# A hybrid transformer layer on one core: S5's filler products, the moment q and k are asked for, and the place of the W2 block sums

## The chip, the core and the metric

The kernel runs on one core of a Trainium2 chip. TensorE (PE) multiplies; VectorE (DVE), ScalarE (ACT) and GpSimd (POOL) do elementwise work; SyncE (SP) mostly issues transfers. The metric is the device time of one launch in microseconds (us): the median of several runs.

## The reference

One layer of a streaming encoder, 1024 tokens, model width 1024, float32. The parts that matter here:

```
h    = rmsnorm(x)
proj = h @ w_in          # u (512) | conv x, B, C | q, k, v (512 each) | forget (8) | gates (3 x 1024)
y_a  = s5(u)             # 32 groups x 16 channels, complex diagonal scan, GELU, GLU
y_b  = B * conv3(C * x_conv)
y_c  = forgetting_attention(q, k, v, f)          # 8 heads x 64, causal
merged = sum_i sigmoid(gates_i) * (y_i @ w_branch_i)
x = x + rmsnorm(merged @ w_out)
x = x + rmsnorm(square(relu(rmsnorm(x) @ w_ff1)) @ w_ff2)
```

## The kernel before, in words

**Stages.** RMSNorm and transposes of x; the projection u; S5's parameters; S5 itself in four quarters of eight groups; V; attention over four head pairs; branch merge and w_out; the two MLP matrices, each by a scheme of seven products of sums of blocks (t_P1 to t_P7 in DRAM), for which the kernel makes sums of blocks of w_ff1 and w_ff2.

**Products.** A float32 weight tile is split into a high and a low part (`split`: ACT copies the high part, DVE subtracts), and each product is three matmuls 128x512. One filler step is three matmuls; a weight tile of 128 columns is 48 matmuls (two halves of 24), and a raw weight load (`r_...`, 1 MB, two buffers) holds two tiles.

**S5's quarter j** (`s5_quarter`, L703 to L818). DVE makes Bt, POOL makes Bx, DVE adds them; PE transposes the sum (pm); ACT copies (Mi). DVE makes CA, POOL makes Cx, DVE adds (CA); PE multiplies (pk), giving Kq and by eight small copies Wi. PE multiplies (px); DVE multiplies by the tables TR and TI (X), scans (Z, eight scans) and multiplies back (S, with Zs from ACT); PE multiplies S and U (py); GELU on ACT and DVE (G, gq); PE multiplies (pz); ACT and DVE finish (so), SP stores (ya). POOL builds the tables for the next quarter meanwhile, from steps of 8 columns to steps of 512 (`s5_tables`).

**What sets the order.** PE's order is written by generators on an estimated clock, `clk`: every matmul adds its cost. `spawn` puts a generator into a heap, `poll` resumes those whose time has come, and `run_with(filler)` (L114) issues one filler step whenever nothing is due. So a `yield SY * 9.0` in `s5_quarter` says how much filler PE gets before the next step of S5. The filler is `proj_stream` (L263): the conv's tiles (cx, cc, cb), then the gates g0 to g22, and q and k of a head pair when asked for (`request_qk`). The next tile is split when the present one has reached a given step. The other engines' order follows from this order of recording, by a list scheduler for most stages; in attention SP's order is as recorded, and before V that of DVE and ACT.

**V and attention.** V's two groups (`v_group`) run behind S5, with the forget gates' chain (`forget`) beside the second; POOL makes the step matrix `stf` for it. Attention (`attention`, around L1104 to L1126) runs 64 units of 128 queries: scores (ps), softmax on DVE and ACT, transposes (pt), products with V (av), all filled by gates' and q/k products. q and k of the next head pair are asked for at unit 12 of each 16.

**W2 sums** (`w2_sums`, L1131 to L1147). Sixteen times: SP reads 1 MB of w_ff2 into w2s (one buffer), POOL makes four differences of blocks 128x512, SP stores four of 256 KB (t_P). In before it starts together with attention.

## Time and profile before

| | us |
|---|---|
| median of 3 runs | 1651.32 |
| lowest, highest | 1644.12, 1651.83 |
| the profiled execution | 1648.08 |
| its span | 1646.3 |
| PE busy | 1603.7 |
| first pm0 | 94.29 |
| py0, py1, py2, py3 | 146.66, 211.28, 273.31, 334.52 |
| W2 sums: first block's read, last store | 427.0, 734.3 |
| head pairs 1, 2 and 3 of attention begin | 559.7, 656.3, 726.4 |

Times in the profile count from the span's start. A row of the timeline is: start, duration, engine, line, operation, output <- inputs, shapes, count; the bracket at its end is the engine's idle time before it and what ended it. A matmul's duration includes its way through the pipeline: two matmuls 128x512 start 0.23 us apart. PEclk is the clock that PE was granted, 1.00 being full. A line can be that of a helper (L65 is any two-input elementwise step), so tiles tell more than lines.

### The profile page before, as it was taken

To read this page: it belongs to the slowest core of one execution; us is meant where nothing else is said; L and a number is where in the kernel's file an instruction comes from. 1 tells how busy PE (TensorE), PEld (TensorE's weight loads), DVE (VectorE), ACT (ScalarE), POOL (GpSimd) and SP (SyncE) were. 2 spreads that over 40 slices of the span, in tenths; PEclk is the share of its full clock that TensorE was granted. 3 is DMA by queue.
4 is the path that set the end of the run, shared out by engine and by line. 5 is a ranking of instruction groups with operands and counts; after the bars stand their busy time and mean duration, and the time that the engine had idled before them with its cause. 6 is when DMAs were issued, how large, how long until landed. Compare 5 with 4: busy or idle time off the path is not lost.

```text
span 1646.3 us, 20948 instructions
## 1 busy us (share of the span) xinstructions
PE 1603.7 (97%) x7783; PEld 1322.8 (80%) x7783; DVE 1033.7 (63%) x1543; ACT 702.9 (43%) x1060; POOL 460.8 (28%) x578
## 2 busy tenths in 40 slices
PE   7999999999999999999999989999999999999997
PEld 6778888889878888777887768888788878888886
DVE  4768666524156463677682874978887674545665
ACT  6223233322254454566343344744445454443442
POOL 1087844100231413120002314444433200101232
PEclk9999999999999999999999999999999999999999
DMA  5412323332463526441873672456554699665521
GB/s 166 125 46 77 105 76 111 91 103 64 145 214 111 196 96 202 131 167 62 282 253 110 216 241 90 149 173 198 184 175 146 202 344 358 236 202 187 186 88 51
DMA packets 186034, 261.73 MB, mean 159 GB/s; under 512 B 24752, under 2 KB 108764, under 8 KB 183884
## 3 DMA queue, kind: packets, MB, share of 16 engines
q1 hardware_dynamic: 170380, 228.93, 43.2%
q10 hardware_dynamic: 15552, 31.46, 5.1%
q8 instruction: 61, 1.00, 0.2%
q14 instruction: 41, 0.34, 0.1%
HBM read 183.54 MB, written 75.63 MB: 157 GB/s over the span
## 4 chain that ended last, share of the span: by engine, by line
PE 42%; DVE 7%; issue 3%; DMA 3%; ACT 3%; POOL 2%; SPq 0%; DVEq 0%; ACTq 0%; POOLq 0%
PE P L122 13%; PE P4f L122 3%; PE P6f L122 3%; PE P7f L122 3%; PE P5f L122 3%; PE P2f L122 3%; PE P3f L122 3%; PE P1f L122 2%; PE wl L122 2%; PE p_g L122 2%; DVE sa L65 1%; PE p_q L122 1%; PE ps L122 1%; PE av L122 1%; PE pt L126 1%
## 5 line engine op out<-in xcount | busy, mean ns | idle before, releaser
L65 DVE TENSOR_TENSOR st<-x,st 128x1024 fp32r<-128x1024 f32 x70 | 86.8, 1251 | 78.5 <-ACT st L73 77.0
L122 PE MATMUL p_g<-hT,w_g_1H 128*128 128x512 f32 x384 | 125.6, 403 | 0.0
L122 PE MATMUL p_g<-hT,w_g_0H 128*128 128x512 f32 x384 | 124.2, 401 | 1.2 <-ACT K L1019 1.2
L73 ACT ACTIVATE st<-x 128x1024 fp32r<-128x1024 f32 x70 | 73.6, 1059 | 99.0 <-PE P6f L122 16.6
L65 POOL TENSOR_TENSOR w2s<-w2s 128x512 f32<-128x512 f32 x32 | 44.5, 1390 | 215.7 <-DMA w2s<-in_w_ff 188.4
L65 POOL TENSOR_TENSOR s<-w1r 128x512 f32<-128x512 f32 x32 | 53.8, 1701 | 145.5 <-DMA w1r<-in_w_ff 114.9
L65 DVE TENSOR_TENSOR sl<-x,sh 128x1024 fp32r<-128x1024 f32 x42 | 56.6, 1352 | 47.4 <-ACT sh L73 47.4
L122 PEld LDWEIGHTS p_g<-hT,w_g_0H 128*128 128x128 f32 x384 | 69.7, 189 | 13.5 <-ACT K L1019 1.6
L122 PE MATMUL pb<-yH,wb_0L 128*128 128x512 f32 x192 | 75.5, 393 | 3.6 <-DVE wb_0L L65 3.6
L122 PEld LDWEIGHTS p_g<-hT,w_g_1H 128*128 128x128 f32 x384 | 69.4, 190 | 11.6 <-issue 0.2
L122 PE MATMUL p_g<-hT,w_g_1L 128*128 128x512 f32 x192 | 75.8, 395 | 0.0
L122 PE MATMUL p_g<-hT,w_g_0L 128*128 128x512 f32 x192 | 75.5, 393 | 0.0
L65 POOL TENSOR_TENSOR fa<-fa,gfin 128x512 f32<-128x512 f32 x16 | 25.5, 1604 | 178.3 <-ACT fjk L1762 178.3
L122 PE MATMUL pb<-yH,wb_0H 128*128 128x512 f32 x192 | 75.2, 392 | 0.0
L122 PE MATMUL pb<-yL,wb_0H 128*128 128x512 f32 x192 | 74.8, 390 | 0.0
L65 DVE TENSOR_TENSOR PT<-pt,PT 128x512 fp32r<-128x512 f32 (+2 forms) x96 | 53.1, 553 | 28.9 <-ACT PT L73 28.4
L73 ACT ACTIVATE PT<-pt 128x512 fp32r<-128x512 f32 (+2 forms) x96 | 46.9, 489 | 53.5 <-PE pt L126 52.4
L73 ACT ACTIVATE sh<-x 128x1024 fp32r<-128x1024 f32 x42 | 44.2, 1058 | 51.4 <-PE P3f L122 9.9
L1056 ACT ACTIVATE P<-ps,mx 128x128 f32<-128x128 f32 (+3 forms) x64 | 47.3, 739 | 28.1 <-DVE mx L1053 28.0
L1053 DVE TENSOR_REDUCE mx<-ps 128x1 f32<-128x128 f32 (+3 forms) x64 | 48.1, 751 | 13.6 <-PE ps L122 13.3
L862 ACT ACTIVATE g<-p_g,bgcol 128x512 f32<-128x512 f32 x48 | 32.8, 682 | 45.8 <-PE p_g L122 45.3
L126 PE MATMUL pt<-ident,P 128*128 128x128 f32 x288 | 48.7, 278 | 3.0 <-DVE PT L65 2.3
(810 smaller groups left out, 4568.0 us busy)
## 6 DMA issues: line engine op xcount, KB each, us to landing
w2s<-in_w_ff SPq DMA_DIRECT2D x16, 1024.0 KB
w1r<-in_w_ff SPq DMA_DIRECT2D x16, 1024.0 KB
as<-sa SPq DMA_DIRECT2D x16, 1024.0 KB
x<-as SPq DMA_DIRECT2D x32, 512.0 KB
x<-t_P SPq DMA_DIRECT2D x32, 512.0 KB
r_g<-in_w_in SPq DMA_DIRECT2D x12, 1024.0 KB
gt_s<-g ACTq DMA_DIRECT2D x48, 256.0 KB
t_P<-w2s SPq DMA_DIRECT2D x48, 256.0 KB
```

The source lines that it names most:

```text
L65: (eng or dve).tensor_tensor(o, x, y, op=op)
L73: act.activation(hi, src, AF.Copy, scale=scale)
L122: pe.matmul(o, l, r, start=start, stop=stop)
L126: pe.transpose(o, i, idn)
L862: act.activation(g, ps, AF.Tanh, bias=bgcol[:, i:i + 1], scale=0.5)
L1053: dve.tensor_reduce(mx, sv, axis=mybir.AxisListType.XY, op=MAX, negate=True)
L1056: act.activation(Pm[:, 0:kend].rearrange("p (c n) -> p c n", c=nch), sv, AF.Exp, bias=mx, accum_out=sm)
```

## The change

1. `run_with` takes a name at which to stop; S5's loop stops when S5 has ended, and later loops poll, so that a generator can go on beside them.
2. S5's yields: 15.0 instead of 9.0 before Bt's add in quarter 0; 8.0 instead of 13.0 (quarter 0) and 1.5 instead of 3.9 (others) before CA's add; 10, 15, 13 and 11 instead of 15 before py.
3. q and k of the next head pair are asked for when the filler left in the present tiles covers the work of the units in front (by durations measured on `clk`), at unit 15 at the latest; such a tile from another raw load is split half a tile later.
4. The W2 sums start in S5's last quarter, behind CA's add (POOL copies one column of CA into the buffer first), make the four differences in place without the second buffer, and pause between V's second group's beginning and the end of `forget`.

The same products and sums are computed. Core of the diff:

```
-        yield SY * (3.9 if j else 9.0)
+        yield SY * (3.9 if j else 15.0)
         tt(Bt, Bt, Bx, ADD)
...
-        yield SY * (3.9 if j else 13.0)
+        yield SY * (1.5 if j else 8.0)
         tt(CA, CA, Cx, ADD)
+        if j == 3:
+            spawn(w2_sums(CA[:, 0, 0, 0:1]))
...
-        yield SY * 15.0
+        yield SY * (10.0, 15.0, 13.0, 11.0)[j]
         py = pp.tile([P, 8, P], F, name=f"py{j}", tag="s", bufs=2)
...
-            if n % 16 == 12 and hp < 3:
+            k = n % 16
+            if k < 8:
+                dur[k] = clk[0] - t0
+            elif hp < 3 and not asked.get(hp) and (k == 15 or ahead_us[0] >= sum(dur[q] for q in range(k - 7, 7))):
+                asked[hp] = True
                 request_qk(hp + 1)
...
+            if i == 0:
+                pool.tensor_copy(w[:, 0, 0, 0:1], after)
+            sp.dma_start(w.rearrange("p k h e -> p k (h e)"), w2_p[:, i])
+            yield 4.5
+            while "v" in ended and "forget" not in ended:
+                yield 1.0
```

How PE's order moves. Counted on it, from one S5 step to the next: 24 more matmuls before pm0; 21 fewer from pm0 to pk0 (51 for 72); 24 fewer from px0 to py0 (78 for 102); 12 fewer from pm to pk in quarters 1 to 3 (21 for 33); px to py 102 as before in quarter 1, 93 for 102 in quarters 2 and 3; 24 for 33 from py3 to pz3. V begins 84 rows earlier, and two tiles (96 matmuls) stand in attention instead: g10 and g12 fill head pair 0, g14 and g16 pair 1, g18 and g20 pair 2. From the second half of the tile q for head pair 3 on, PE, ACT, DVE and SP have the same order in both.

PE around the first transposes, before (p_cc is a conv product, pm S5's transposes of Bt):

```order
322 L122 MATMUL p_cc_00_1103<-hT_172,w_cc_0H 128x512
323 L122 MATMUL p_cc_00_1103<-hT_173,w_cc_0H 128x512
324 L122 MATMUL p_cc_00_1103<-hT_172,w_cc_0L 128x512
325 L126 MATMUL pm_1114<-ident,Bt_1016 128x128 x8
326 L122 MATMUL p_cc_00_1103<-hT_174,w_cc_0H 128x512
327 L122 MATMUL p_cc_00_1103<-hT_175,w_cc_0H 128x512
```

and the same place after:

```order
346 L124 MATMUL p_cc_01_1138<-hT_176,w_cc_0H 128x512
347 L124 MATMUL p_cc_01_1138<-hT_177,w_cc_0H 128x512
348 L124 MATMUL p_cc_01_1138<-hT_176,w_cc_0L 128x512
349 L128 MATMUL pm_1152<-ident,Bt_1019 128x128 x8
350 L124 MATMUL p_cc_01_1138<-hT_178,w_cc_0H 128x512
351 L124 MATMUL p_cc_01_1138<-hT_179,w_cc_0H 128x512
```

The transposes stand 24 rows later, inside the second half of the same weight tile.

DVE in quarter 1, before (X from px, w_cb the split of a weight tile, ac the conv, Z the scans):

```order
282 L65 TENSOR_TENSOR X_1885<-px_1875,TI_1269 64x1024 x2
283 L65 TENSOR_TENSOR X_1884<-px_1875,TR_1268 128x1024
284 L65 TENSOR_TENSOR X_1884<-X_1884,X_1885 128x1024
285 L65 TENSOR_TENSOR w_cb_0L<-r_cb_1953,w_cb_0H 128x1024
286 L65 TENSOR_TENSOR ac_1779<-ac_1779,bs_1906 128x1024
287 L777 SCALAR_TENSOR_TENSOR Z_1912<-r_505,X_1884 128x128 x8
```

and after:

```order
280 L65 TENSOR_TENSOR X_1846<-px_1836,TI_1275 64x1024 x2
281 L65 TENSOR_TENSOR X_1845<-px_1836,TR_1274 128x1024
282 L65 TENSOR_TENSOR X_1845<-X_1845,X_1846 128x1024
283 L65 TENSOR_TENSOR w_cc_0L<-r_cc_1890,w_cc_0H 128x1024
284 L65 TENSOR_TENSOR vp_1829<-vp_1829,xs_1660 128x1024
285 L60 TENSOR_SCALAR ac_1886<-vp_1829,cwcol 128x1024
286 L68 SCALAR_TENSOR_TENSOR ac_1886<-vp_1829,cwcol,ac_1886 128x1024 x2
287 L809 SCALAR_TENSOR_TENSOR Z_1866<-r_505,X_1845 128x128 x8
```

Before, the split of w_cc, the add vp and the conv's three taps stood ahead of X, and two other steps stood between X and the scans; now those five stand between.

POOL behind the last quarter's Cx, after (w2s is a block of w_ff2, stf the step matrix for V):

```order
238 L65 TENSOR_TENSOR Cx_2663<-C2t,pii_515 128x8x16 x9
239 L683 COPY w2s_2692<-CA_2662 128x1
240 L65 TENSOR_TENSOR w2s_2692<-w2s_2692 128x512 x4
241 L65 TENSOR_TENSOR w2s_2827<-w2s_2827 128x512 x4
242 L65 TENSOR_TENSOR w2s_2948<-w2s_2948 128x512 x4
243 L969 MEMSET stf 128x1024
```

Before, Cx was followed by stf at once, and the sums came behind four memsets for attention. On SP's queue the first block's read stands, after, right behind quarter 2's stores and ahead of the load r_g6 and of the eight Wi copies of quarter 3; the load r_wv0 (for V's second group) stands behind the fourth block's read. The last block's stores stand ahead of the load r_q2, so all sixteen blocks are through before head pair 2.

More of the change, by code (lines that the diff above doesn't have):

```diff
@@ L112, in settle, with run_with @@
             poll()
-    def run_with(filler):
-        while events:
+    ended = set()
+    def run_with(filler, until=None):
+        while events and until not in ended:
             if events[0][0] > clk[0] and next(filler, DONE) is DONE:
@@ L261, in proj @@
             yield
+    ahead_us = [0.0]
     def proj_stream():
@@ L282, in proj_stream @@
                 poll()
+            late = nxt is not None and nxt.ready is not None and nxt.raw is not cur.raw
             for th in range(2):
                 for kt, _ in enumerate(proj(cur, th)):
-                    if nxt is not None and (th, kt) == (0, 5):
+                    if nxt is not None and (th, kt) == ((1, 0) if late else (0, 5)):
                         nxt.split()
+                    ahead_us[0] = 0.64 * (15 - 8 * th - kt + 16 * (nxt is not None))
                     yield
@@ L666, in hybrid_layer, with w2_sums @@
     gp = es1.enter_context(pool_("gp", side="right"))
+    w2_es = ExitStack()
+    w2p = w2_es.enter_context(pool_("w2p", side="right"))
+    def w2_sums(after):
+        w2_p = a["w_ff2"].rearrange("(i k p) e -> p i k e", p=P, k=2)
+        for i in range(16):
+            w = w2p.tile([P, 2, 2, HALF], F, name=f"w2s{i}", tag="w2s")
+            if i == 0:
[4 more added lines that the diff above has]
+                yield 1.0
+            b11, b12, b21, b22 = w[:, 0, 0], w[:, 0, 1], w[:, 1, 0], w[:, 1, 1]
+            tt(b11, b12, b11, SUB, pool)
+            tt(b12, b22, b12, SUB, pool)
+            tt(b22, b22, b11, SUB, pool)
+            tt(b21, b21, b22, SUB, pool)
+            yield 6.5
+            for m, src in (("P5", b11), ("P7", b12), ("P6", b22), ("P4", b21)):
+                sp.dma_start(t_s[m][i // 4][:, i % 4], src)
+            yield 3.0
     PX = 5.0
@@ L875, in s5_all @@
             yield from s5_quarter(j)
+        ended.add("s5")
     s5_tables(0)
     spawn(s5_all(), 0)
-    run_with(ps_)
+    run_with(ps_, "s5")
     while any(t.name[0] == "c" for t in todo) or len(todo) > 21:
         next(ps_)
+        poll()
     cv_es.close()
@@ L921, in hybrid_layer @@
             next(ps_)
+            poll()
         split(wv[1][1], wv[1][2], wv[1][0])
@@ L924, in hybrid_layer @@
             next(ps_)
+            poll()
         split(wv[0][1], wv[0][2], wv[0][0])
         for _ in v_group(1):
-            pass
+            poll()
     zfl = zf.rearrange("p t h -> p (t h)")
@@ L979, in forget @@
             sp.dma_start(cum_s[2 + k], cmn[:, k, :])
+        ended.add("forget")
+    ended.add("v")
     spawn(forget(), 1.0)
     vg = v_group(0)
-    run_with(vg)
+    run_with(vg, "forget")
     for _ in vg:
-        pass
+        poll()
     vc_es.close()
@@ L1105, in attention @@
         prev = None
+        dur, asked, t0 = {}, {}, 0.0
         for n, u in enumerate(units):
@@ L1113, in attention @@
                 yield 4.0
+                t0 = clk[0]
             scores(u)
@@ L1119, in attention @@
                 yield from tail(prev)
-            if n % 16 == 12 and hp < 3:
+            k = n % 16
[3 more added lines that the diff above has]
+                asked[hp] = True
                 request_qk(hp + 1)
+            t0 = clk[0]
             prev = u
@@ L1127, in hybrid_layer @@
     FILL_A, FILL_B = 1.1, 0.6
-    def w2_sums():
-        w2_p = a["w_ff2"].rearrange("(i k p) e -> p i k e", p=P, k=2)
-        yield 4.0
-        for i in range(16):
-            w = at.tile([P, 2, 2, HALF], F, name=f"w2s{i}", tag="w2s")
-            t2 = at.tile([P, HALF], F, name=f"w2t{i}", tag="w2t")
-            sp.dma_start(w.rearrange("p k h e -> p k (h e)"), w2_p[:, i])
-            yield 7.0
-            b11, b12, b21, b22 = w[:, 0, 0], w[:, 0, 1], w[:, 1, 0], w[:, 1, 1]
-            tt(b11, b12, b11, SUB, pool)
-            tt(t2, b22, b11, SUB, pool)
-            tt(b12, b22, b12, SUB, pool)
-            tt(b21, b21, t2, SUB, pool)
-            yield 9.0
-            for m, src in (("P5", b11), ("P6", t2), ("P7", b12), ("P4", b21)):
-                sp.dma_start(t_s[m][i // 4][:, i % 4], src)
-            yield 3.0
     with tc.manual_schedule(engines={mybir.EngineType.SP}):
         spawn(attention())
-        spawn(w2_sums())
         run_with(ps_)
     es3.close()
+    w2_es.close()
     ext = ctx.enter_context(pool_("ext"))
```

## The prediction

> **What bounds the kernel now.** I read the page first: it says which engine is full.
>
> ```profile
> span 1646.3 us, 20948 instructions
> PE 1603.7 (97%) x7783; PEld 1322.8 (80%) x7783; DVE 1033.7 (63%) x1543; ACT 702.9 (43%) x1060; POOL 460.8 (28%) x578
> ```
>
> TensorE is busy for all but 42.6 us (1646.3 − 1603.7). The change adds and removes no product, so it can win only idle time of PE and time in which PE runs slowly. The list of PE's waits says where the idle time lies; I show those that fall inside the part that is reordered.
>
> ```profile
> PE pm L126 <- DVE Bt L65: 4.3, 2, 3.8
> PE pt L126 <- DVE PT L65: 2.3, 3, 1.5
> PE pv L122 <- ACT g L862: 0.8, 1, 0.8
> ```
>
> The columns are total, times, longest. 7.4 us in all: 4.3 before S5's transposes pm, 2.3 before attention's transposes pt, 0.8 at V's start. Then the windows, for the clock and for where the attention's waits fall. Behind the length and each engine's busy time stand the granted clock (PEclk), the DMA share and GB/s; the last three windows hold head pairs 1, 2 and 3, each from its first scores on.
>
> ```profile
> 50.00:100.00 50.00, 46.22 (x204) 35.79 (x204) 41.43 (x202) 11.83 (x17) 12.45 (x37) 0.93 0.35 101
> 559.70:656.30 96.60, 95.91 (x508) 78.33 (x507) 51.75 (x93) 46.98 (x95) 27.16 (x20) 1.00 0.45 153
> 656.30:726.40 70.10, 67.77 (x382) 54.62 (x382) 47.41 (x90) 39.70 (x85) 15.27 (x11) 1.00 0.46 144
> 726.40:790.00 63.60, 61.70 (x369) 49.77 (x368) 49.28 (x94) 39.97 (x82) 5.11 (x4) 1.00 0.33 114
> ```
>
> Head pair 1 has 0.69 us of PE idle, pair 2 has 2.33, pair 3 has 1.90. Everything from the scores of head pair 3 (726 us) on stands in the same order on PE before and after, so I add nothing there.
>
> **pm0: the gain that is surest.** TensorE's timeline around the first transposes:
>
> ```profile
> 89.67 0.62 PE L122 MATMUL p_cc<-hT,w_cc_0H 128*128 128x512 f32 x2
> 90.13 0.39 PE L122 MATMUL p_cc<-hT,w_cc_0L 128*128 128x512 f32 x1
> 94.29 1.94 PE L126 MATMUL pm<-ident,Bt 128*128 128x128 f32 x8 [3.78 <-DVE Bt L65]
> 95.88 1.20 PE L122 MATMUL p_cc<-hT,w_cc_0H 128*128 128x512 f32 x2
> ...
> 99.87 0.63 PE L122 MATMUL p_cc<-hT,w_cc_0H 128*128 128x512 f32 x2
> ```
>
> Two products start 0.46 us apart, so one takes 0.23 us (0.2268 over long stretches). The wait is 3.78 us. Behind it PE is slow: from 95.88 to 99.87 it starts nine products, 3.99 us where 2.04 would do (+1.95), and the eight transposes take 1.59 us from start to next start, at half pace, so 0.8 at full (+0.8; pm1, quoted below, is busy 1.03 us against 1.94 here). The clock of 0.93 in the 50 to 100 window says the same (7% of 50 us is 3.4 us of missing clock). The wait thus costs 3.78 + 2.75 = 6.5 us. What it waited for, on DVE:
>
> ```profile
> 92.91 1.23 DVE L65 TENSOR_TENSOR Bt<-Bt,Bx 128x1024 f32<-128x1024 f32 x1 [2.79 <-POOL Bx L65]
> 105.38 1.60 DVE L65 TENSOR_TENSOR CA<-CA,Cx 128x1152 f32<-128x1152 f32 x1 [6.25 <-POOL Cx L65]
> ```
>
> Bt is done at 94.14. The change puts 24 more products ahead of pm0: PE is busy until 90.13 + 0.23 + 24 × 0.2268 = 95.8, so the wait goes with 1.7 us to spare. What is late next is pk0, which needs CA (done 106.98): 95.8 + 0.8 + 51 × 0.2268 = 108.2, 1.2 us to spare. **−6.5**; if the slow stretch had come without the wait, only −3.8.
>
> Here the Trainium skill has a rule, in "TensorE: Matmul & The Clock Gate", section "What's actually happening": the clock halves after an idle activity window of about 3.4 us, and the windows run free of the program. The trace agrees in kind: 3.78 us of waiting, then products at half pace. What speaks against this change is that any new wait of some us may bring it back; that is priced by rows below.
>
> **S5's later steps.** The removed 96 products stand between S5's steps: from pm0 on, 21 fewer before pk0, 24 fewer before py0, 12 fewer in each later pm→pk, 9 fewer in px2→py2, px3→py3 and py3→pz3. Each was cover for a chain on DVE, ACT and POOL, so each gap is checked.
>
> py0, first the PE rows, then POOL and DVE:
>
> ```profile
> 121.72 1.95 PE L122 MATMUL px<-U,Mi 128*128 128x128 f32 x16
> 146.66 0.38 PE L122 MATMUL py<-S,CA 128*128 128x128 f32 x2
> 120.62 2.13 POOL L65 TENSOR_TENSOR TI<-pt 128x512 f32<-128x512 f32 x1
> 128.86 2.95 DVE L777 TENSOR_TENSOR_SCAN Z<-r,X 128x128 f32<-128x128 f32 x8
> 137.04 1.20 DVE L65 TENSOR_TENSOR S<-S,Zs 128x1016 f32<-128x1016 f32 x1
> ```
>
> px0 will start at 108.2 + 7.4 = 115.6 (24 products between, as now, 5.4, and pk's 16 short matmuls, 2.0 as px's). py0 then comes 24.94 − 24 × 0.2268 = 19.5 us later, at 135.1. But X needs table TI, which POOL ends at 122.75 and which nothing in the change moves forward. So S, done at 138.24 now, gains at most the 1.1 us between 122.75 and the X of today (123.87), and some rearrangement around the scans; I take 136.8. **+1.7** (0 to 3.1).
>
> py1, in the same way:
>
> ```profile
> 173.84 1.03 PE L126 MATMUL pm<-ident,Bt 128*128 128x128 f32 x8
> 186.35 1.95 PE L122 MATMUL px<-U,Mi 128*128 128x128 f32 x16
> 211.28 0.38 PE L122 MATMUL py<-S,CA 128*128 128x128 f32 x2
> 195.36 1.04 POOL L65 TENSOR_TENSOR pt<-TR,wr 128x512 f32<-128x512 f32 x1
> 202.94 1.28 POOL L65 TENSOR_TENSOR TI<-pt 128x512 f32<-128x512 f32 x1
> 188.99 2.46 DVE L65 TENSOR_TENSOR X<-px,TI 64x1024 f32<-64x1024 f32 x2
> 186.31 2.67 DVE L68 SCALAR_TENSOR_TENSOR ac<-vp,cwcol,ac 128x1024 f32<-128x1024 f32 x2
> 200.77 5.32 DVE L777 TENSOR_TENSOR_SCAN Z<-r,X 128x128 f32<-128x128 f32 x8
> 209.68 1.21 DVE L65 TENSOR_TENSOR S<-S,Zs 128x1016 f32<-128x1016 f32 x1
> ```
>
> The group of all 32 scans:
>
> ```profile
> L777 DVE TENSOR_TENSOR_SCAN Z<-r,X x32: 394/421/1444, 128.9 to 319.9; 128x128 f32<-128x128 f32 x32
> ```
>
> S is ready at 210.89, PE arrives at 211.28: 0.4 us of slack. The eight scans took 5.32 us here and 2.95 in the quarter before, where POOL did small table steps. A scan takes 0.4 us by the group's minimum and median and up to 1.44: beside POOL's 512-wide steps (195.36 to 204.2) I take 1.25, otherwise 0.4. POOL's tables keep their distance to pm1, but px1 comes 12 × 0.2268 = 2.7 us sooner after pm1 (9.8 us instead of 12.5). In the new order DVE does the X steps at once (2.0 for px, then 2.46 and two of 1.25), and then a split, an add and three taps of the conv (two taps are 2.67; 1.2, 1.3 and 0.8 for the others), so the scans start 13 us after px1, 22.8 after pm1. POOL's wide steps last from 21.5 to 30.4 after pm1: six scans at 1.25 and two at 0.4 make 8.3 us. Then 6.0 us up to S (the same steps as 206.12 to 210.89, and one 1.2 us conv add that now stands among them). S comes 27.3 us after px1, PE after 24.9. **+2.4** (0, if the scans fall behind POOL's steps, to 4.5, if all eight are slow and POOL's own steps stretch).
>
> The rest of S5, and V's start:
>
> ```profile
> 268.71 1.21 DVE L65 TENSOR_TENSOR S<-S,Zs 128x1016 f32<-128x1016 f32 x1
> 273.31 0.38 PE L122 MATMUL py<-S,CA 128*128 128x128 f32 x2
> 235.85 1.06 PE L126 MATMUL pm<-ident,Bt 128*128 128x128 f32 x8 [0.54 <-DVE Bt L65]
> 345.61 1.61 PE L122 MATMUL pz<-gq,BD 128*128 128x128 f32 x13
> 342.72 1.29 DVE L68 SCALAR_TENSOR_TENSOR gq<-G,py 128x512 f32<-128x512 f32 x2 [1.35 <-ACT G L800]
> ```
>
> The 0.5 us before pm2 goes, since py1's wait gives Bt2 time (−0.5, or 0). pz3 has 345.61 − 344.01 = 1.6 us of slack and loses 9 × 0.2268 = 2.0: +0.4. V's tiles now stand together, so the 0.8 us behind ACT's g goes (−0.8, or 0). py2 loses 2.0 of its 3.4 us (273.31 − 269.92) and stays free; py3 loses as much, and in the last quarter POOL has no tables to build beside the scans.
>
> **The W2 sums.** POOL's rows in head pair 2, with DVE's neighbour:
>
> ```profile
> 658.49 2.26 POOL L65 TENSOR_TENSOR w2s<-w2s,w2t 128x512 f32<-128x512 f32 x1
> 657.34 2.27 DVE L65 TENSOR_TENSOR w_q_0L<-r_q,w_q_0H 128x1024 fp32r<-128x1024 f32 x1 [3.66 <-ACT w_q_0H L73]
> 661.70 0.66 PE L126 MATMUL pt<-ident,P 128*128 128x128 f32 x4 [1.50 <-DVE PT L65]
> 670.13 1.23 DVE L65 TENSOR_TENSOR w_q_1L<-r_q,w_q_1H 128x1024 fp32r<-128x1024 f32 x1
> ```
>
> DVE's split beside POOL's subtract took 2.27 us, and PE then waited 1.50. After the change all 16 blocks are through before head pair 2, and 96 more products fill the attention, its q and k in one piece. Of the 0.69 + 2.33 us idle in pairs 1 and 2, I take all of pair 2's and little of pair 1's, where sums still run: −2.5 (0 to −3.0).
>
> Moved to S5's end, the sums meet G3 and gq3 on DVE. The Trainium skill ("SBUF — State Buffer", section "Who interferes with whom") states that POOL and a DVE instruction with two SBUF inputs lock each other out for a whole instruction. The 2.27 and 2.26 us above agree with it. By that rule each step of the chain that meets a sum would wait up to the whole subtract. By rows alone a meeting costs 2.27 − 1.23 (the next split) = 1.0 us, and with pz3 already late each meeting counts; two are possible, one is my guess at half: +0.5 (0 to 2.1).
>
> On SP's queue the first block's read waits for POOL's copy, hence for CA3, and r_g6, the Wi3 copies and r_g8 stand behind it; r_wv0 and r_q0 stand behind later blocks' reads, each of which waits for the stores of the block before. g6 is used 95 rows after pk3 on PE, over 19 us; I take +0.2 for all of these (0 to 3). POOL's mask for V (stf) stands behind three blocks, and DVE needs it ahead of V's first weight split; from pk3 to V PE has 256 rows, over 50 us, and a block's four subtracts are some 5 us (four of 1.3, or 2.26 at worst), so it is in time: 0.
>
> **The sum.** Gains 6.5 + 0.5 + 0.8 + 2.5 = 10.3. Losses 1.7 + 2.4 + 0.4 + 0.5 + 0.2 = 5.2. The profiled execution took 1648.08 us (span 1646.3 and 1.8 around it): 1648.1 − 5.1 = **1643.0**. It lies 3.2 us under the median of the runs shown (1651.32, with 1644.12 as the lowest), so this is 0.5% under the median and 0.3% under the execution it is summed against. What a measurement of this kernel can tell from no change is about 0.5%, 8.3 us.
>
> **Rivals.** *The chains hold (0.22):* S5's steps have more slack than I see, since DVE's work moves forward too. Then the losses are 0.2 to 1 us and the time is near 1638. For it: S1's chain has 6 us of movable conv work in it. Against: TI's end at 122.75 does not move.
>
> *Nothing is won (0.22):* py0 and py1 wait near their upper ends (3.1 + 4.5), pz3 2.5, and the attention keeps its 3 us of idle time, because they belong to its chain and not to the sums. Gains of 7.8 (6.5, 0.5, 0.8) stand against losses of 10.1: 1650. For it: head pair 3, with no sums beside it, waits about as long as pair 2 (1.90 us, with POOL at 5.11 us of its 63.6).
>
> *S5's chain halves the clock again (0.08):* the mechanism is a wait at py0 and at py1 long enough to fill most of a clock window; it decides from about 2.3 us of idle time in one (3.78 did it at pm0). Each costs 2.75 us besides itself. With the upper ends above and no attention gain: 1650 + 2 × 2.75 = 1656, slower than before; with a late load in SP's queue (3) 1659. For it: my 2.4 at py1 stands at that point. Against: both waits must fall unluckily in the windows.
>
> *The order moves and time does not (part of the second):* idle time moves from pm0 to py0 and py1 one for one, and the time stays at 1648.
>
> **How the numbers follow.** My forecast has 0.48, with its own range 1639 to 1648 (py0 and py1 from 0.8 under to 2 over, attention 0 to 3). The range is to hold 8 times in 10: it reaches down to 1636 in the first rival and up to 1652 in the second. Faster by over 0.5% means under 1643.06: half of the forecast's 0.48, nearly all of the first rival's, none of the others': 0.45. Slower means over 1659.6: the far end of the third rival, and mishaps beyond the rows: 0.05. Within: 0.50.
>
> **What would show it.** Right: no wait before pm0 and a clock of 1.00 from 50 to 100; waits of 1 to 3 us before py0 and py1 on DVE's S; scans of about 8 us in quarter 1; no wait before pt in head pair 2; POOL's last block before it. Wrong: pm0 waits or the half clock appears elsewhere in S5; py0 and py1 run on without a wait; pair 2 waits as now; ACT or DVE waits for r_g6, r_wv0 or r_q0.

## The result and the profile after

The changed kernel takes 1660.11 us (median of 6 runs, 1658.2 to 1664.77); the kernel before, beside it, takes 1649.88 (6 runs). The ratio is 1.0069, with a 95% interval of 1.0054 to 1.0083: 0.7% slower. The forecast was 1643.0, and the range ended at 1652. The sign was wrong.

The page of the changed kernel has 10.8 us more of span, and PE 5.4 us longer busy with the same 7783 matmuls:

```profile
span 1657.1 us, 20915 instructions
PE 1609.0 (97%) x7783; PEld 1327.5 (80%) x7783; DVE 1031.8 (62%) x1543; ACT 704.1 (42%) x1060; POOL 454.3 (27%) x579
```

The list of PE's waits answers to the rows of before. The 4.3 us before pm are down to 0.3; the new rows are py, p_cx and the V products pv, and pt has grown.

```profile
PE py L124 <- DVE S L65: 7.6, 2, 3.9
PE pt L128 <- DVE PT L65: 3.8, 2, 3.5
PE pv L124 <- DVE V L65: 2.2, 2, 1.3
PE p_cx L124 <- ACT bs L880: 2.1, 1, 2.1
PE pm L128 <- DVE Bt L65: 0.3, 1, 0.3
```

The windows show the clock (the third figure from the end). The 0.93 of before in 50 to 100 is gone, and four other windows now have 0.97 where before had 1.00: each of the four long waits above brought back a stretch at half clock.

```profile
50.00:100.00 50.00, 50.00 (x233) 39.23 (x233) 41.42 (x202) 12.78 (x19) 12.18 (x36) 1.00 0.36 101
100.00:150.00 50.00, 46.11 (x228) 38.69 (x227) 33.12 (x42) 12.98 (x16) 47.18 (x72) 0.97 0.26 70
200.00:250.00 50.00, 47.94 (x247) 40.12 (x247) 33.41 (x48) 15.73 (x19) 25.39 (x54) 0.97 0.31 90
250.00:300.00 50.00, 46.30 (x225) 38.95 (x224) 26.20 (x41) 13.81 (x16) 21.63 (x31) 0.97 0.29 87
450.00:500.00 50.00, 45.64 (x245) 37.06 (x244) 29.90 (x58) 24.41 (x53) 17.52 (x13) 0.97 0.66 221
```

To set two orders against each other I count, for the start of a step in each trace, the filler matmuls (p_...) ahead of it, take off 0.2268 us for each, and compare with the trace of before. What is left is time lost (+) or won (−), stage by stage. For py0: 139.59 − 429 × 0.2268 = 42.29 after, 146.66 − 450 × 0.2268 = 44.59 before. For the changed kernel, in us:

| stage | lost or won |
|---|---|
| up to px0 (pm0's wait and its slow stretch) | −6.4 |
| px0 to pm1 (py0) | +6.7 |
| pm1 to pm2 (py1) | +3.2 |
| pm2 to pm3 (py2) | +5.7 |
| pm3 to V's first product | +0.3 |
| V and the first q and k, up to the first scores | +0.9 |
| head pair 0 | +6.2 |
| head pair 1 | −0.5 |
| head pair 2 | −2.6 |
| the rest (same order on PE in both) | −2.6 |
| sum | +10.8 |

The last row has no change in it. All but four of the 18 profiles taken later are also quicker there than the profile of before, by up to 3.0 us, so it belongs to that one profile. Single profiles of one kernel differ by a few us, and a stage is to be read with that in mind.

**py0.** POOL's and DVE's rows of the changed kernel, and PE's:

```profile
115.29 3.24 POOL L65 TENSOR_TENSOR pt<-TR,wr 128x512 f32<-128x512 f32 x1
123.10 1.29 POOL L65 TENSOR_TENSOR TI<-pt 128x512 f32<-128x512 f32 x1
```

```profile
115.29 1.20 DVE L65 TENSOR_TENSOR w_cb_0L<-r_cb,w_cb_0H 128x1024 fp32r<-128x1024 f32 x1
124.43 2.46 DVE L65 TENSOR_TENSOR X<-px,TI 64x1024 f32<-64x1024 f32 x2 [6.80 <-POOL TI L65]
138.24 1.20 DVE L65 TENSOR_TENSOR S<-S,Zs 128x1016 f32<-128x1016 f32 x1
```

```profile
139.59 0.69 PE L124 MATMUL py<-S,CA 128*128 128x128 f32 x2 [3.89 <-DVE S L65]
```

The same POOL step and the same split of DVE in the kernel before:

```profile
115.02 1.04 POOL L65 TENSOR_TENSOR pt<-TR,wr 128x512 f32<-128x512 f32 x1
120.06 1.56 DVE L65 TENSOR_TENSOR w_cb_0L<-r_cb,w_cb_0H 128x1024 fp32r<-128x1024 f32 x1 [1.50 <-ACT w_cb_0H L73]
```

PE had nothing left to do at 135.7. DVE idled 6.8 us for POOL's table TI, which ended at 124.39, 1.6 later than before: POOL's first wide step took 3.24 us where the same step took 1.04 before, and two full-width steps of DVE, the split and a conv add, moved forward by the change, now lay beside it. (Before, they lay beside TI itself, which took 2.13 there and 1.29 here.) The half clock behind the wait and a late Bt cost another 2.6.

**The quarter of py1.** DVE, ACT and PE:

```profile
194.24 7.18 DVE L809 TENSOR_TENSOR_SCAN Z<-r,X 128x128 f32<-128x128 f32 x8
205.95 1.21 DVE L65 TENSOR_TENSOR S<-S,Zs 128x1016 f32<-128x1016 f32 x1
```

```profile
201.52 1.06 ACT L812 ACTIVATE Zs<-Z 64x1024 f32<-64x1024 f32 x1 [9.50 <-DVE Z L809]
203.67 0.60 ACT L880 ACTIVATE bs<-p_cb 128x512 f32<-128x512 f32 x1
```

```profile
204.32 1.06 PE L124 MATMUL p_cx<-hT,w_cx_0H 128*128 128x512 f32 x2 [2.06 <-ACT bs L880]
```

The scans fell beside POOL's wide steps as forecast and took 7.18 us; S was ready 27.95 us after px1 (179.21). But PE did not wait at py1. It waited earlier, in the filler: ACT's copy bs, which frees a PSUM buffer of the products, stands behind Zs on ACT, and Zs waits for the scans. Filler cannot cover a chain when its own consumer is queued behind that chain.

**py2.** Here ACT's row comes first, then DVE's, then PE's.

```profile
254.30 1.06 ACT L73 ACTIVATE w_g_1H<-r_g 128x1024 fp32r<-128x1024 f32 x1 [4.52 <-PE p_g L124]
```

```profile
255.39 1.81 DVE L65 TENSOR_TENSOR w_g_1L<-r_g,w_g_1H 128x1024 fp32r<-128x1024 f32 x1 [4.76 <-ACT w_g_1H L73]
257.13 6.38 DVE L809 TENSOR_TENSOR_SCAN Z<-r,X 128x128 f32<-128x128 f32 x8
```

```profile
268.39 0.46 PE L124 MATMUL py<-S,CA 128*128 128x128 f32 x2 [3.70 <-DVE S L65]
```

The split in the kernel before, on ACT and on DVE:

```profile
250.83 1.06 ACT L73 ACTIVATE w_g_1H<-r_g 128x1024 fp32r<-128x1024 f32 x1 [3.51 <-PE p_g L122]
253.97 1.24 DVE L65 TENSOR_TENSOR w_g_1L<-r_g,w_g_1H 128x1024 fp32r<-128x1024 f32 x1
```

Between X and the scans DVE has the split of a weight tile to do. It waits for ACT's half of the split, and that waits for PE's filler. px2 now comes 45 filler matmuls earlier in the stream (768 ahead of it, 813 before), the filler that releases the split does not, and so DVE stood still for 4.76 us inside the S5 chain. Before, ACT's half was done at 251.89, while DVE was still at X, and DVE did not wait.

**Head pair 0.** SP, ACT and PE:

```profile
475.27 4.68 SPq L695 DMA_DIRECT2D t_P<-w2s  x4
481.87 0.38 SPq L684 DMA_DIRECT2D w2s<-in_w_ff  x1
482.30 1.09 SPq L233 DMA_DIRECT2D r_q<-in_w_in  x2
```

```profile
488.68 1.06 ACT L73 ACTIVATE w_q_0H<-r_q 128x1024 fp32r<-128x1024 f32 x1 [4.51 <-DMA r_q<-in_w_in]
```

```profile
491.65 1.11 PE L128 MATMUL pt<-ident,P 128*128 128x128 f32 x4 [3.55 <-DVE PT L65]
```

The same split in the kernel before:

```profile
495.33 1.06 ACT L73 ACTIVATE w_q_0H<-r_q 128x1024 fp32r<-128x1024 f32 x1 [0.86 <-PE p_g L122]
```

q's load stands behind the stores of one W2 block and the read of the next, and the read has to wait until the stores have left the buffer. ACT reached q's split first and stopped, with the softmax behind it on ACT and DVE.

### The profile page after: what moved, and what is told of

Its sections match the earlier page's. It is cut to its first block, busy times and chain, and to the rows that moved or that the text cites. A ratio compares the mean times of both kernels' runs of the same rounds, so it can differ in the third digit from the quotient of the medians.

```text
span 1657.1 us, 20915 instructions
## 1 busy us (share of the span) xinstructions
PE 1609.0 (97%) x7783; PEld 1327.5 (80%) x7783; DVE 1031.8 (62%) x1543; ACT 704.1 (42%) x1060; POOL 454.3 (27%) x579
## 4 chain that ended last, share of the span: by engine, by line
PE 70%; DVE 6%; DMA 3%; POOL 3%; ACT 3%; issue 2%; SPq 0%; DVEq 0%; ACTq 0%; POOLq 0%
PE P L124 16%; PE p_g L124 13%; PE pb L124 4%; PE p_q L124 3%; PE P4f L124 3%; PE P7f L124 3%; PE P3f L124 3%; PE P5f L124 3%; PE P2f L124 3%; PE P6f L124 3%; PE P1f L124 2%; PE wl L124 2%; PE av L124 2%; PE ps L124 2%; PE pt L128 2%
## 5 line engine op out<-in xcount | busy, mean ns | idle before, releaser
L65 POOL TENSOR_TENSOR w2s<-w2s 128x512 f32<-128x512 f32 x64 | 87.0, 1360 | 160.8 <-DMA w2s<-in_w_ff 157.0
L73 ACT ACTIVATE sh<-x 128x1024 fp32r<-128x1024 f32 x42 | 44.2, 1058 | 51.4 <-PE P3f L124 9.9
## 6 DMA issues: line engine op xcount, KB each, us to landing
x<-as SPq DMA_DIRECT2D x32, 512.0 KB, 10.8
```

The lines of the kernel that those rows point to most:

```text
L65: (eng or dve).tensor_tensor(o, x, y, op=op)
L73: act.activation(hi, src, AF.Copy, scale=scale)
```

## The experiments

The theory formed from this trace (A): S5 loses where a gap became shorter than the chain in it; V and attention lose where a W2 block stands in the way, as a load's predecessor on SP's queue or as POOL's subtracts beside DVE. The first rival (B) was that the early sums or the asking rule make S5's loss as well; later rivals stand with each run. Times of one run are named so; the others have their ratio to the kernel before.

### One part alone, one part undone

Bt's number alone:

```
 (kernel before)
-        yield SY * (3.9 if j else 9.0)
+        yield SY * (3.9 if j else 15.0)
         tt(Bt, Bt, Bx, ADD)
```

> The kernel before with one number changed: 15.0 instead of 9.0 ahead of Bt's add in quarter 0, so 24 more matmuls ahead of pm0 and every other gap of S5 with as many as before. Theory A (the changed kernel loses its time in gaps that were made shorter): pm0's wait and the slow stretch behind it go, 6.4 us as in the changed kernel (its pm0 to pk0 stretch), nothing comes back at py0, py1 or py2: 1649.9 - 6.4 = 1643.5. Theory B (the wait only moves to py0, because POOL's table ends at a fixed time): S5 gives the 6.4 back by py1 and the time stays at 1648 to 1650.

Measured: 1656.44, ratio 1.0036 (1.0021 to 1.0051), slower. S5 behaved as theory A said: −5.4 by px0, nothing given back up to V, V another −2.5, so 8.3 us ahead at the first scores. Then head pair 2 lost 15.7. Its waits and the split of q there:

```profile
PE pt L126 <- DVE PT L65: 12.8, 9, 5.2
```

```profile
663.13 1.06 ACT L73 ACTIVATE w_q_0H<-r_q 128x1024 fp32r<-128x1024 f32 x1 [4.44 <-DMA r_q<-in_w_in]
```

q's load came late there too; moreover q and k of pair 3 were used up as filler amid pair 2 (120 filler products stood in it instead of 165), and four of its last five units ran bare. Neither theory had that: the filler that S5 takes is missing in attention.

All three of S5's yields alone:

```
 (kernel before)
-        yield SY * (3.9 if j else 9.0)
+        yield SY * (3.9 if j else 15.0)
...
-        yield SY * (3.9 if j else 13.0)
+        yield SY * (1.5 if j else 8.0)
...
-        yield SY * 15.0
+        yield SY * (10.0, 15.0, 13.0, 11.0)[j]
```

> The kernel before with the three changes of S5's yields and nothing else (the W2 sums start with attention, q and k are asked for at unit 12). Theory A (S5's shorter gaps make the loss): waits before py0 and py2 of about 3.9 us each, one at or ahead of py1 of about 2, each followed by a stretch at half clock of about 2 us; by py3 9 us behind the kernel before; in all 1657 to 1661. Theory B (the W2 sums' early start makes the loss, by DVE's and SP's queues): S5 keeps its gain of pm0 and the time is 1641 to 1646.

Measured: 1659.56 (one run). By stage −6.2, +7.6, +2.7, +7.0: S5 loses in the same places as in the changed kernel, without the early sums and with the old asking rule. Theory A; B falls for S5.

S5's yields back, the rest as changed:

```
 (changed kernel)
-        yield SY * (3.9 if j else 15.0)
+        yield SY * (3.9 if j else 9.0)
...
-        yield SY * (1.5 if j else 8.0)
+        yield SY * (3.9 if j else 13.0)
...
-        yield SY * (10.0, 15.0, 13.0, 11.0)[j]
+        yield SY * 15.0
```

> The changed kernel with all of S5's yields as before: only the W2 sums' place and the time at which q and k are asked for differ from the kernel before. Theory A: pm0's wait is back (6.4 us lost against the changed kernel), the waits ahead of py0, py1 and py2 are gone, V loses 1 to 2.5 us to POOL beside DVE's chain of the forget gates, head pair 0 up to 6 us where its q load is late, pairs 1 and 2 win 3: 1648 to 1655. Theory B (these two parts make most of the loss): 1657 or more.

Measured: 1651.72 (one run). S5 is level with before in each stage (−0.1 to 0.0). V loses 7.9, pair 0 2.0, pair 2 wins 2.4. So the changed kernel's small V loss (0.9) was not what the early sums cost as such.

### Which gap makes which wait

py's yields back:

```
 (changed kernel)
-        yield SY * (10.0, 15.0, 13.0, 11.0)[j]
+        yield SY * 15.0
```

> The changed kernel with 15.0 ahead of py in all quarters, as before (102 matmuls from px to py again). Theory A: py0's wait (3.9) and its slow stretch (2.1) go, py2's 3.9 shrinks by the 2.0 that 9 more matmuls cover or goes, the loss ahead of py1 stays (its gap was not shortened): 1660 - 6.5 - 2 to 5 = 1648.5 to 1651.5. Theory B (the 21 and 12 matmuls fewer from pm to pk are what uncovers DVE): py0 and py2 wait about as long as in the changed kernel and the time is over 1656.

Measured: 1656.07 (one run). py0's wait and py2's went (py2's quarter +0.3 instead of +5.7), but 5.0 came back around py0, where pz0 waited 2.6 for gq. The loss ahead of py1, which A had staying, shrank to 0.7 (3.2 in the changed kernel). The total missed A's figure, because V lost 7.2.

CA's yields back:

```
 (changed kernel)
-        yield SY * (1.5 if j else 8.0)
+        yield SY * (3.9 if j else 13.0)
```

> The changed kernel with CA's yields as before (72 matmuls from pm0 to pk0, 33 from pm to pk later), py's as changed (78 from px0 to py0, 93 to py2 and py3). Theory A (py0's wait needs both cuts together, since POOL's table ends at a fixed time and px0 alone decides how much of it is left; py2's comes from 12 fewer ahead of pk2, which lets px2 overtake the split of the g tile that stands between X and the scans): no wait at py0, at the p_cx products in quarter 1, or at py2; a wait of up to 3 before pz0 as in the candidate; S5 ends 3 to 6 us ahead of before. Theory B (each cut ahead of py costs by itself): py0 waits 1 to 4 and py2 2 to 4 and S5 ends behind before.

Measured: 1643.17 (one run). No wait at py0 or in py1's quarter, 1.3 at py2, 2.9 at pz0, S5 1.3 us ahead of before at py3: less than the 3 to 6 expected, but A's waits are where A put them. Quarter 0 and the other quarters apart:

```
 (changed kernel, first run)
-        yield SY * (1.5 if j else 8.0)
+        yield SY * (1.5 if j else 13.0)
 (changed kernel, second run)
-        yield SY * (1.5 if j else 8.0)
+        yield SY * (3.9 if j else 8.0)
```

> The changed kernel with 13.0 again ahead of CA's add in quarter 0 only (72 matmuls from pm0 to pk0); 1.5 in the other quarters and py as changed. Theory A (py0's wait hangs on quarter 0's cut, the waits at the p_cx products and at py2 on the cuts of quarters 1 and 2): no wait at py0, 3 us at pz0 as with all of CA's yields restored; the p_cx or py1 loss of 3 to 4 and py2's loss of 5 to 6 stay; S5 ends 2 to 6 us behind before. Theory B (quarter 0's cut shifts everything that follows, and the later waits follow from it): S5 ends ahead of before by 1 or more, as with all restored.

> The counterpart: 3.9 again ahead of CA's add in quarters 1 to 3, 8.0 in quarter 0, py as changed. Theory A: py0's wait and its slow stretch stay (about 6.5 us with pm1); no loss at py1, at most 1.5 at py2; S5 ends level with before to 1.5 behind. Theory B (quarter 0's cut brings the later waits too): losses ahead of py1 and py2 as in the changed kernel, S5 ends 8 or more behind.

Measured: 1660.41 and 1659.09 (one run each). With quarter 0's gap back, py0's wait is gone and py2's quarter still loses 4.0, py1's 0.8. With the others back, quarter 0 loses 7.7 in full, py1's quarter 1.3, py2's 0.6. Each cut makes the wait of its own quarter, mostly; py1's loss needs both (3.2 with both cuts, 0.8 and 1.3 with one). S5 ended 5.6 and 4.7 us behind before at V; A had 2 to 6 and at most 1.5. Both kernels lost nearly 10 us in V.

### Where the sums stand

The sums started with attention:

```
 (changed kernel)
-        if j == 3:
-            spawn(w2_sums(CA[:, 0, 0, 0:1]))
...
-            if i == 0:
-                pool.tensor_copy(w[:, 0, 0, 0:1], after)
...
         spawn(attention())
+        spawn(w2_sums(None), 4.0)
```

> The changed kernel with the W2 sums started with attention, as before; S5's yields and the asking for q and k as changed. Theory A (the 6.2 us lost in head pair 0 come from the q load standing behind a block's read, which waits for that block's buffer, so they hang on where the sums stand): S5 loses its 9.5 us as in the changed kernel, V loses nothing, head pair 0 loses 0 to 1, pair 2's gain of 2.6 shrinks to 0 to 1: 1654 to 1657. Theory B (the new moment of asking makes the load late): pair 0 loses about 6 again and the time is 1660 to 1663.

Measured: 1656.69 (one run). V −1.7, pair 0 +3.2 (half of what it was), pair 2 −2.3. So pair 2 keeps its gain although POOL's sums run on to 667.8, 22 us into it. Two reasons for the gain can be told apart in other runs: with S5's yields back, pair 2 has 165 filler products as before, the sums are through at 562.0, and it gained 2.4; with S5's yields alone it has 267, the sums run on to 734.8, and it gained 1.6. So either seems enough, by one run each. The changed kernel has both, and which of them carried it there is not shown.

The old moment of asking:

```
 (changed kernel)
-                    if nxt is not None and (th, kt) == ((1, 0) if late else (0, 5)):
+                    if nxt is not None and (th, kt) == (0, 5):
...
-            k = n % 16
-            if k < 8:
-                dur[k] = clk[0] - t0
-            elif hp < 3 and not asked.get(hp) and (k == 15 or ahead_us[0] >= sum(dur[q] for q in range(k - 7, 7))):
-                asked[hp] = True
+            if n % 16 == 12 and hp < 3:
                 request_qk(hp + 1)
```

> The changed kernel with q and k asked for at unit 12 again, and split at the old step; all else as changed. Theory A (pair 0's loss is the load behind the sums' reads): a request at another moment meets the SP queue at another phase; S5 keeps +9.5, pair 0 loses 0 to 6, and pair 2 has q's products only where the old rule puts them. 1655 to 1662. Theory B (the new rule is what makes pair 2 quick): pair 2 loses its gain of 2.6 and up to 10 more, as in the kernel with Bt's number alone, whose q for pair 3 was used up amid pair 2 and left it without products: 1662 to 1672.

Measured: 1660.49 (one run). PE, ACT, DVE, POOL and SP have the same instructions in the same order as in the changed kernel: with these yields the new rule asks where the old one did. So this run is a second execution of one program. B falls, because the new rule changes nothing in the changed kernel; what the rule does where it asks at another moment is not tested. The run also says how far two executions agree: from pm3 on every stage is within 0.2 of the changed kernel, S5 had lost 1.5 more by then, 1.3 of it in py2's quarter.

POOL as issuer of the sums' transfers:

```
 (changed kernel)
-            sp.dma_start(w.rearrange("p k h e -> p k (h e)"), w2_p[:, i])
+            pool.dma_start(w.rearrange("p k h e -> p k (h e)"), w2_p[:, i])
...
-                sp.dma_start(t_s[m][i // 4][:, i % 4], src)
+                pool.dma_start(t_s[m][i // 4][:, i % 4], src)
```

> The changed kernel with the W2 sums' reads and stores issued by POOL instead of SP, so that nothing of theirs stands ahead of other loads on SP's queue; their place and the asking rule as changed. Theory A (head pair 0's 6.2 us are q's load held up on SP's queue behind a block's stores and the next block's read, with ACT and DVE standing still at the split of q): pair 0 loses 0 to 1 instead of 6.2; S5 loses its 9.5 as in the changed kernel; V 0 to 3: 1653 to 1657. Theory B (POOL's subtracts beside DVE make pair 0's and V's losses): pair 0 and V lose as in the changed kernel, 1659 to 1663.

Measured: 1688.48 (one run). Pair 0's loss fell to 2.8, but V lost 30.9. The longest of PE's waits is for V's weight split on DVE, ahead of which DVE needs POOL's mask, and on POOL the mask stood among blocks that waited for their transfers:

```profile
PE pv L124 <- DVE wvL L65: 22.6, 1, 22.6
```

```profile
381.22 0.97 POOL L969 MEMSET stf<- 128x1024 f32 x1
```

In the changed kernel POOL wrote it at 347.07.

So this run does not tell A from B. Next one load alone was moved, q's of pair 1, from SP to ACT:

```
 (changed kernel)
-                    sp.dma_start(self.t[:, :, o:o + w], w_in_k[:, :, c0:c0 + w])
+                    (act if self.name == "q1" else sp).dma_start(self.t[:, :, o:o + w], w_in_k[:, :, c0:c0 + w])
```

> The changed kernel with one thing moved: q's load for head pair 1 is issued by ACT instead of SP; the W2 sums, their transfers and all yields as changed. Theory A (pair 0's 6.2 us are that load held up behind a block's stores and the next block's read on SP's queue): the load starts some 13 us sooner, ACT does not wait at q's split, and pair 0 loses 0 to 2; all else as in the changed kernel: 1654 to 1657. Theory B (pair 0's loss is POOL beside DVE): pair 0 loses 5 to 7 again and the time stays at 1659 to 1662.

Measured: 1660.94 (one run). ACT's rows:

```profile
470.43 4.00 ACTq L233 DMA_DIRECT2D r_q<-in_w_in  x2
488.30 1.06 ACT L73 ACTIVATE w_q_0H<-r_q 128x1024 fp32r<-128x1024 f32 x1 [0.21 <-PE p_g L124]
```

The load started 12 us sooner, and the split did not wait for it any more. But the issue itself held ACT for 4.00 us, and pair 0 still lost 4.4, in waits of 1.2 and less, more than A's 2; the time lies in B's range. The other profiles speak against B as the larger part: in the ten other runs in which at least 20 of POOL's subtracts fell into pair 0 and ACT did not wait there for q's load, pair 0 lost between −0.6 and 3.2. Where ACT waited 4.4 us or more for it in a head pair (pair 0 of the changed kernel and of its second execution, pair 2 of three other runs), that pair lost 5.4 to 15.7. In between stands the run with py's yields back: ACT waited 1.95, and pair 0 lost 5.3. The late load made the 3.55 us wait and, behind it, the half clock, which 0.97 over 50 us puts at 1.5; the rest of pair 0's loss stays open.

### Candidates

S5 shortened only where runs had shown slack, with the sums at attention and early:

```
 (changed kernel; both)
-        yield SY * (1.5 if j else 8.0)
+        yield SY * (13.0, 3.9, 1.5, 1.5)[j]
...
-        yield SY * (10.0, 15.0, 13.0, 11.0)[j]
+        yield SY * (10.0, 15.0, 15.0, 8.0)[j]
 (the first: also the sums started with attention, as above)
```

> A candidate. 24 more matmuls ahead of pm0 as changed, but S5 shortened only where the runs so far showed slack: 13, 3.9, 1.5, 1.5 ahead of CA's add and 10, 15, 15, 8 ahead of py (px0 to py0 78 matmuls with pm0 to pk0 at 72 again, py3 earlier); new asking rule; the W2 sums start with attention. Theory A (a gap costs only where it is shorter than the chain in it): S5 gains 5 to 6.5, V 0 to 1, attention 0 to 2 either way: 1641 to 1646. Theory B (any shortening of S5 comes back as waits of about its size, since splits in the queues of DVE and ACT follow PE's products): S5 loses as many as it wins, 1649 to 1655.

> The same candidate with the W2 sums in S5's last quarter, as changed. Theory A (the sums beside V's chain of the forget gates cost what the lock between POOL and DVE makes of it, 1 to 8 us by where they fall): S5 gains 5 to 6.5, V loses 1 to 8, pair 2 gains 2.5: 1641 to 1651, and slower than the same with the sums at attention if V loses over 2.5. Theory B (the early sums cost nothing, and only S5's gaps did): V loses under 1: 1639 to 1643.

Measured: 1653.39, ratio 1.0014 (1.0003 to 1.0024), and 1659.82, ratio 1.0052 (1.0031 to 1.0072). Both were outside A's figures. The first lies in B's range, but not by B's step: S5 was still 3.1 us ahead of before at V. In the second it was 2.0 behind, 4.1 of it lost between pm3 and V, where it waited 0.9 at pz3 and 2.8 at V's start. pz0 waited 2.9 us in both. In the first, DVE's seven CA steps behind py0 took 5.99 beside POOL's wide steps, 2.59 in the kernel before, and G for pz0 is queued behind them:

```profile
147.24 5.99 DVE L65 TENSOR_TENSOR CA<-C1t,prr 128x128 f32<-128x128 f32 x7
153.14 0.68 DVE L62 TENSOR_SCALAR G<-G 128x1024 f32<-128x1024 f32 x1
```

The first lost 5.4 in pair 2 (q's load again, ACT waiting 5.34), the second 13.4 in V. The same with 12.5, 15, 15, 8 ahead of py and POOL issuing the transfers, early and at attention:

> Candidate: 24 more matmuls ahead of pm0; CA 13, 3.9, 1.5, 1.5 and py 12.5, 15, 15, 8; W2 sums from S5's last quarter, their transfers issued by POOL; asking rule as changed. Theory A (gaps that hold, and SP's queue free): S5 gains 6, V loses 0 to 3 (POOL beside DVE's chain of the forget gates), pair 0 nothing, pair 2 gains 2.5: 1640 to 1646. Theory B (the sums' place itself costs): V loses 5 or more and the time is 1648 or more.

> The same candidate with the W2 sums started with attention, transfers issued by POOL. Theory A: S5 gains 6, V 0 to 2, pairs 0 and 1 nothing, pair 2 gains 2.5, since q's load no longer waits: 1638 to 1643. Theory B (the 5.2 us that the candidate with the sums at attention lost in pair 2 come from POOL's subtracts, not from SP's queue): pair 2 loses about 5 again and the time is 1645 to 1650.

Measured: 1689.13, ratio 1.0234 (1.0219 to 1.025), and 1789.23, ratio 1.0843 (1.0825 to 1.0861). Both failed by the order of POOL: V lost 44.2 in the first, and in the second the blocks stood in among S5's POOL steps:

```profile
PE pm L128 <- DVE Bt L65: 121.4, 4, 49.5
```

They tell nothing of q's load. Then CA as before and py between:

```
 (changed kernel)
-        yield SY * (1.5 if j else 8.0)
+        yield SY * (3.9 if j else 13.0)
...
-        yield SY * (10.0, 15.0, 13.0, 11.0)[j]
+        yield SY * (12.5, 15.0, 15.0, 11.0)[j]
```

> The changed kernel with CA's yields as before and 12.5, 15, 15, 11 ahead of py (90 matmuls from px0 to py0, 102 to py1 and py2). Theory A: pz0's wait of 2.9 with its slow stretch and py2's 1.3 go, so S5 ends 5 to 6.3 us ahead of before; whether q's loads in V and in attention meet the sums on SP's queue is open (0 or 5 to 8 each): 1640 to 1645 if none does, 1646 to 1653 if one does. Theory B (S5's waits come whenever the W2 sums and the asking are as changed): S5 gains 3 or less.

Measured: 1647.31, ratio 0.9978 (0.9969 to 0.9988): the best version, 0.2% faster than before. py0, py1 and py2 have no wait; S5 is 4.5 us ahead at V, half a microsecond less than expected, since 2.8 still go between py0 and pz0 (PE waits 1.91 there for ACT's copy bs, and half clock follows). Pair 2 wins 2.6, and V loses 9.5. SP and ACT there:

```profile
401.14 0.38 SPq L684 DMA_DIRECT2D w2s<-in_w_ff  x1
401.57 1.09 SPq L233 DMA_DIRECT2D r_q<-in_w_in  x2
```

```profile
408.06 1.06 ACT L73 ACTIVATE w_q_0H<-r_q 128x1024 fp32r<-128x1024 f32 x1 [7.98 <-DMA r_q<-in_w_in]
```

It is the mechanism of pair 0, now in V: q's first load right behind a block's read, ACT at its split for 7.98 us, V's products behind it. To remove both, the same S5 with the sums at attention, held back while a load of q is asked for and not recorded:

```
 (the version above, sums started with attention)
     def request_qk(hp):
+        qpend[0] = True
...
                 n = sum(w for _, w in self.parts)
+                if self.name[0] == "q":
+                    qpend[0] = False
...
             yield 6.5
+            while qpend[0]:
+                yield 0.6
...
             yield 3.0
+            while qpend[0]:
+                yield 0.6
```

> The mended S5 (24 more matmuls ahead of pm0; CA's yields as before; 12.5, 15, 15, 11 ahead of py), the new asking rule, the W2 sums in place but started with attention, and held back while a load of q and k is asked for and not yet recorded, so that q's load stands ahead of a block's stores on SP's queue. Theory A (two causes: S5's gaps and q's load behind the blocks on SP's queue): S5 gains 4.5 to 6, V loses nothing, no head pair waits for q's load, pairs lose 0 to 1 each and pair 2 gains 2.5: 1640 to 1645. Theory B (V's and attention's losses are POOL's subtracts beside DVE, wherever they stand): pairs 0 to 2 lose 5 or more in all and the time is 1648 or more.

Measured: 1653.59, ratio 1.0023 (1.0011 to 1.0035). V won 1.5, pair 0 lost 0.5 and pair 1 2.5, but pair 2 lost 8.4. Its rows:

```profile
638.25 1.23 DVE L65 TENSOR_TENSOR w_g_1L<-r_g,w_g_1H 128x1024 fp32r<-128x1024 f32 x1 [3.04 <-ACT w_g_1H L73]
```

```profile
673.19 1.14 SPq L235 DMA_DIRECT2D r_q<-in_w_in  x2
```

```profile
677.91 1.06 ACT L73 ACTIVATE w_q_0H<-r_q 128x1024 fp32r<-128x1024 f32 x1 [9.86 <-DMA r_q<-in_w_in]
```

That split freed the load buffer at 639.5; the load was issued at 673.19. The hold works on the estimated clock, and by then SP's queue was three blocks behind it. So q's load was still late and theory A has not been refuted by this run, but the cure that I wrote for it failed.

Last, the kernel with CA's yields as before, with rounds:

> The changed kernel with CA's yields as before, once more with rounds, since one run came out at 1643.2 and its profile had q's first load waited for by ACT (2.5 us) but not by PE. Theory A (undoing this one part of the change takes back the loss): 1642 to 1647, faster than before by 0.2 to 0.5%. Theory B (the single run was a good one): 1649 or more.

Measured: 1649.83, ratio 0.9994 (0.9982 to 1.0005): no difference from before; the single 1643.17 lies under all ten of these (1646.85 to 1651.77). Its two profiles are of one program and differ in V by 6.4 us (−1.4 and +5.0): in the slower one PE waited 3.00 for V, and half clock followed. The forget gates' chain on DVE, seven steps of 64 columns, in the quick one and then in the slow one:

```profile
400.45 1.77 DVE L68 SCALAR_TENSOR_TENSOR lg<-lg,s 128x64 f32<-128x64 f32 x7
```

```profile
401.07 6.06 DVE L68 SCALAR_TENSOR_TENSOR lg<-lg,s 128x64 f32<-128x64 f32 x7
```

and POOL's block beside them:

```profile
404.12 6.29 POOL L65 TENSOR_TENSOR w2s<-w2s 128x512 f32<-128x512 f32 x4 [9.68 <-DMA w2s<-in_w_ff]
```

```profile
401.69 5.37 POOL L65 TENSOR_TENSOR w2s<-w2s 128x512 f32<-128x512 f32 x4 [7.21 <-DMA w2s<-in_w_ff]
```

A block that comes at 404.12 misses the chain, one that comes at 401.69 lies on it. This fits the lock that the Trainium skill describes ("SBUF — State Buffer", section "Who interferes with whom"), and the trace agrees: the small steps take 0.25 us each without POOL and nearly 0.9 beside it. The pause in the change was made for this, but it stops what is recorded, not what is queued.

The V stage over all runs with SP issuing the early sums: +0.9 (the changed kernel), +7.2, +7.9, +1.0, +13.4, −1.4, +5.0, +9.5, +2.1, +9.7, +9.9. With the sums started at attention: −2.5, −1.3, −1.7, −2.2, −1.5. So the early sums cost V some 2 to 16 us against the late ones in all but one of these executions, and the changed kernel stands near the low end. Two mechanisms make it. In the four with +7.2, +9.5, +9.7 and +13.4, ACT waited 8.0 to 13.9 us at its split for q's first load, and PE 6.4 to 7.9 for V; in the +5.0 ACT did not wait, and the forget gates' chain was the one that was stretched. In the +7.9 and +9.9 ACT waited 5.6 and 4.6 and PE in several places; these are not taken apart here. In the changed kernel neither was hit: its seven steps took 1.78 us and ACT did not wait.

## Why the prediction was wrong

The forecast was 5.1 us less than before, the profiles show 10.8 more. Of the 15.9 us between them pair 0 makes 6.2, py2 5.7, py0 5.0, V 1.7 and py1's quarter 1.3; the other stages, the unchanged one among them, take 4 off again.

- *pm0* was right: 6.5 forecast, 6.4 measured, 3.7 of it up to pm0 (the wait) and 2.7 from there to pk0 (the half clock).
- *py0* had the right place and the wrong size: +1.7 forecast (0 to 3.1), 3.9 of wait and 2.6 behind it. The step that failed is "which POOL ends at 122.75 and which nothing in the change moves forward": nothing moved it forward, but DVE's steps moved beside POOL's wide ones and pushed it back to 124.39, which is 1.6 of the 2.6 us by which S came later than the 136.8 forecast. The slow stretch behind the wait was kept for a rival.
- *py1*: the chain was right (scans 8.3 forecast, 7.18 measured; S 27.3 and 27.95 us after px1), the place of the wait was not: ACT's in-order queue stopped the filler, at 2.1, and the clock added 1.7.
- *py2* "stays free" failed, and it is the largest error in S5: 5.7 us. I compared S's slack with the missing products, but DVE's queue holds a split between X and the scans that follows the filler, not px2. Cutting filler ahead of px moves px against every instruction that is released by filler. (The gaps that the prediction lists add up to 108 products fewer, not 96; nothing in the sum hangs on it.) The run with py's gap back and the run with CA's back took this loss to 0.3 and 1.7.
- *The rest of S5* was right: pm2 −0.7 (−0.5 forecast), pz3 +0.2 (+0.4).
- *The sums* were the step "I take +0.2 for all of these (0 to 3)" on SP's queue. q's first load was named, the one for pair 1 was not, and the loads' slack was checked only for g6. Pair 0 lost 6.2, of which pair 1's late load made the 3.55 us wait and the half clock behind it. For V −0.8 was forecast, and nothing for POOL beside the forget gates' chain or for a late q; the changed kernel lost 0.9, other phases up to 13.4, so that V came out this low was luck.
- *Pair 2* was right in size (−2.5 and −2.6). The prediction named two reasons, the sums gone and more filler; by one run each, either is enough alone; which one did it is not shown.
- *The clock.* The third rival, S5's chain halving the clock again, is the one that came, at 8%; with its upper ends it gave 1656 to 1659, and 1660 was measured; that this is so near is partly luck, since it held nothing for py2 and too much for py1. I asked for about 2.3 us of idle time in one window. No run shows such a limit: waits of 1.68 to 2.06 us were followed by half clock, others of 2.62 to 2.85 were not (the rows stand in the last section). Waits of 2.06, 3.55, 3.70 and 3.89 us each brought 50 us of the changed kernel to 0.97. A chance of this should have been part of the sum: each of the two waits that I forecast myself stood at a size at which it can happen.

## What to carry to other kernels

Filler between two steps of a chain isn't only time: other queues advance by it. Before gaps are shortened, list for each engine what stands between the chain's steps and what releases it, and check the distance to the chain, not the slack of its last result. A background job with a buffer of its own on a shared in-order queue costs by where it falls on the chip, not where a simulated clock puts it: two executions of one program differed by 6.4 us in V, where a block came 2.4 us earlier.
